# Five buffers of upper weight parts 64 bytes apart modulo 512, lower parts 320 bytes further

## The chip, the cores and the metric

The kernel runs on one core of a Trainium2 chip. The metric is the device time of one execution in microseconds (us). Engines are named as the profile names them: PE is the matrix engine, PEld its loading of stationary operands, DVE the vector engine, ACT the scalar engine, POOL the general engine, SP the engine whose queue issues most of the DMAs. Two runs of the kernel before took 1813.53 and 1813.9 us, median 1813.72 us.

## The reference

One encoder layer in float32 on 256 tokens of width 2048: a half-step feed-forward block, a mixer, a second half-step feed-forward block, each between two RMS norms.

```
D_MODEL = 2048; SEQ = 256; D_FF = 5632; HGRN_WIDTH = 1024; ATTN_WIDTH = 1024; KV_WIDTH = 256
def swiglu(x, w_gate_up, w_down):
    gate, up = jnp.split(x @ w_gate_up, 2, axis=-1)
    return (jax.nn.silu(gate) * up) @ w_down
...
ff = swiglu(rms_norm(x, pre_norm_ffn1), w_ffn1_gate_up, w_ffn1_down)
x = x + 0.5 * rms_norm(ff, post_norm_ffn1)
h = rms_norm(x, pre_norm_mix)
q_h, i_h, f_fwd, f_bwd, g_h, q_a, k_a, v_a = jnp.split(h @ w_mix_in, split_at, axis=-1)
y_h = hgrn2_mixer(q_h, i_h, f_fwd, f_bwd, g_h, ...)      # gated recurrence, chunks of 64 tokens
y_a = window_attention(q_a, k_a, v_a, attn_sink, rel_bias_table)
x = x + rms_norm(concatenate([y_h, y_a]) @ w_mix_out, post_norm_mix)
ff = swiglu(rms_norm(x, pre_norm_ffn2), w_ffn2_gate_up, w_ffn2_down)
x = x + 0.5 * rms_norm(ff, post_norm_ffn2)
```

The weights are read once each; nearly all arithmetic is in the products with the gate/up weights (2048 x 11264), the down weights (5632 x 2048), the mixer's input weights (2048 x 6656) and its output weights (2048 x 2048).

## The kernel before, in words

**Products in three parts.** PE takes float32r operands, which keep fewer bits than float32. So every operand x is split into an upper part (a float32r copy) and a lower part (x minus the upper part), and a product is the sum of three matmuls: upper by upper, upper by lower, lower by upper (`three`, lines 450 to 466, the matmul itself at line 458; `products_N`, lines 375 to 381). In `three` the activations (tiles `xt`, `ht`, `xs`, `sp`, `yh`, `ya`) are stationary and the weight parts (`h`, `l`) stream past them, 512 columns at a time. In the mixer's projections (`proj_T_pieces`, lines 326 and 331) it is the other way about: the weight parts are stationary, 128 columns each, and the activations stream.

**Splitting.** A weight tile arrives by DMA in a `raw` tile of 2048 float32 per partition. Each half of it goes through `split_half` and `split_act`: ACT copies 1024 values into an `h` tile (line 177), DVE subtracts and writes an `l` tile (line 178).

```python
    def split_half(raw, i, hp=hip, lp=lop):
        part = raw[:, i * 1024 : (i + 1) * 1024]
        h = hp.tile([P, 1024], F32R, tag="h", name=nm("h"))
        l = lp.tile([P, 1024], F32R, tag="l", name=nm("l"))
        split_act(h, l, part)
```

The pools `hip` and `lop` have five buffers each, used in turn for the whole kernel. Some of the blocks are multiplied by a Strassen-like scheme of seven products in place of eight (`seven`, `products`), whose first block comes from small tiles elsewhere (`h1`, `l1`, `ha`, `la`, `first`).

**Order of the work.** PE, DVE and ACT run in an order written out by hand (`tc.manual_schedule`). The order in which SP issues the weights' DMAs follows from the buffers that come free.

**Where tiles begin.** Pools lie one after another in a partition of the on-chip memory, and a tile's start is the sum of what was allocated before it. In this text the phase of a tile is its start address in a partition, in bytes, modulo 512. The matmul operands are slices of tiles that begin at multiples of 512 bytes within them, so an operand has its tile's phase. Before the change `X`, the three lasting `raw` buffers, all ten `h` and `l` buffers, `xt`, `ht`, `xs`, `sp`, `h1`, `l1`, `ha` and `la` have phase 64. Two tiles that nothing reads fill space, one of 416 bytes (`line`, in the pool `stat`, which follows `lop`) and one of 416 bytes (`shim`, at the far end). Tiles of the pool `mid`, in which the mixer's own work goes on, have phase 416: among them `kT`, `qh` and the pair `cum0`/`cum1`, which twice holds the parts of a first block (named `first` in the trace). The other `first` tiles have phase 64.

Of the kernel before, what the change touches and what calls it, by code (L numbers as in the profile page):

```python
# [11 lines left out]
F32 = mybir.dt.float32  # L12
# [8 lines left out]
P = 128  # L21
# [12 lines left out]
REL_W = 512  # L34


@with_exitstack
def hymba_layer_kernel(
    ctx: ExitStack,
# [26 lines left out]
    const = ctx.enter_context(tc.tile_pool(name="const", bufs=1))  # L66
    xp = ctx.enter_context(tc.tile_pool(name="xp", bufs=1))
    rawp = ctx.enter_context(tc.tile_pool(name="rawp", bufs=3))
    hip = ctx.enter_context(tc.tile_pool(name="hip", bufs=5))
    lop = ctx.enter_context(tc.tile_pool(name="lop", bufs=5))  # L70
    psum = ctx.enter_context(tc.tile_pool(name="psum", bufs=4, space=bass.MemoryType.PSUM))
    dram = ctx.enter_context(tc.tile_pool(name="dram", bufs=1, space=bass.MemoryType.DRAM))
# [30 lines left out]
    nc.vector.memset(mhalf, -0.5)  # L103
    stat = ctx.enter_context(tc.tile_pool(name="stat", bufs=4))

    stat.tile([P, 104], F32, tag="line", name="line", bufs=1)

    def to_columns(srcs, tag, eng):

# [239 lines left out]
    class LeadN:  # L349


        def __init__(self, w, c0, slot):
            self.w, self.c0, self.slot = w, c0, slot
# [2027 lines left out]
```

## Time and profile before

| what | us |
|---|---|
| median of the runs (two) | 1813.72 |
| span of the profiled execution, first to last instruction | 1810.8 |
| PE busy | 1799.0 (99%) |
| PEld busy | 1494.3 (83%) |
| DVE busy | 1660.0 (92%) |
| ACT busy | 1134.9 (63%) |
| POOL busy | 182.8 (10%) |

How to read it: the span is the time between the first and the last instruction of the profiled execution. The time of a run also holds what lies around the span, 1813.7 - 1810.8 = 2.9 us by the median. The granted PE clock averaged 0.999 of full speed. Matmuls overlap each other, so that a matmul's own duration in a row (some 390 ns) is longer than the step from one matmul's start to the next; the step is what adds up to the span. A row of the timeline or of the chain that holds several matmuls in sequence gives it.

### The profile page before, as it was taken

The numbers are of one execution on the slowest core, as the hardware profiler recorded it, in microseconds if no ns is written. First come the engines' busy times: TensorE is split into PE (matmuls) and PEld (weight loads), VectorE is DVE, ScalarE is ACT, GpSimd is POOL, SyncE is SP. The second block draws the span as 40 slices with busy tenths as digits, with TensorE's granted clock in tenths as the row PEclk, the third lists the DMA queues.
The fourth block names the chain that finished last, engine by engine and source line by source line (L and its number), as shares of the span: only waits on it lengthen the run. The fifth ranks groups of instructions, "written<-read, shape, count | busy, mean of one in ns | idle before, by whom it ended". The sixth has DMA issues, their size and how long they took to land.

```text
span 1810.8 us, 23729 instructions
## 1 busy us (share of the span) xinstructions
PE 1799.0 (99%) x8400; PEld 1494.3 (83%) x8400; DVE 1660.0 (92%) x2179; ACT 1134.9 (63%) x1508; POOL 182.8 (10%) x172
## 2 busy tenths in 40 slices
PE   9999999999999999999999999999999999999998
PEld 7888888888888888888888888888888888888886
DVE  7999999999999998988898898899999999999997
ACT  7565666665665767566676666566666666566663
POOL 1011111111011110110000100111111111011110
PEclk9999999999999999999999999999999999999999
DMA  8889999998699997964655767889999998699994
GB/s 301 248 239 283 273 286 257 248 261 255 214 319 315 301 281 251 296 166 164 175 171 162 243 206 274 256 234 271 284 269 271 255 250 247 190 326 341 270 321 166
DMA packets 218423, 459.16 MB, mean 254 GB/s; under 512 B 13128, under 2 KB 49824, under 8 KB 217024
## 3 DMA queue, kind: packets, MB, share of 16 engines
q1 hardware_dynamic: 181600, 389.07, 61.6%
q0 software_dynamic: 36528, 68.30, 22.1%
q8 instruction: 66, 1.08, 0.2%
q14 instruction: 53, 0.43, 0.1%
q10 hardware_dynamic: 176, 0.27, 0.0%
HBM read 442.89 MB, written 14.70 MB: 253 GB/s over the span
## 4 chain that ended last, share of the span: by engine, by line
PE 96%; DVE 2%; ACT 1%; issue 0%; DMA 0%; DVEq 0%; POOL 0%; ACTq 0%; POOLq 0%
PE pa L458 44%; PE pb L458 38%; PE pa L326 5%; PE pa L331 3%; PE pa L381 1%; PE pa L380 1%; PE pa L379 1%; DVE l L178 1%; PE pb L1728 1%; PE pa L1172 1%; PE pb L1172 1%; PE pb L2029 0%; PE pb L2003 0%; DMA slots<-in_w_mix_out_dram 0%; PE pb L211 0%
## 5 line engine op out<-in xcount | busy, mean ns | idle before, releaser
L177 ACT CAST h<-raw 128x1024 fp32r<-128x1024 f32 (+1 forms) x850 | 835.1, 1012 | 428.2 <-PE pb L458 132.2
L178 DVE TENSOR_TENSOR l<-raw,h 128x1024 fp32r<-128x1024 f32 (+1 forms) x850 | 964.3, 1168 | 76.2 <-ACT h L177 56.4
L458 PE MATMUL pa<-h,xt 128*128 128x512 f32 x1194 | 418.9, 392 | 0.1
L458 PE MATMUL pb<-h,xt 128*128 128x512 f32 x1038 | 371.2, 392 | 0.1
L458 PEld LDWEIGHTS pa<-h,xt 128*128 128x128 f32 x1194 | 224.1, 188 | 48.0 <-DVE xt L233 0.6
L458 PEld LDWEIGHTS pb<-h,xt 128*128 128x128 f32 x1038 | 194.8, 188 | 46.5 <-DVE pb L1236 3.7
L458 PE MATMUL pa<-l,xt 128*128 128x512 f32 x597 | 233.0, 390 | 0.1
L458 PE MATMUL pb<-l,xt 128*128 128x512 f32 x519 | 202.2, 390 | 0.0
L1011 POOL DMA_DIRECT2D raw<-in_w_ffn_gate_up_dram x78 | 94.5, 1212 | 732.0 <-DVE l L178 679.6
L458 PE MATMUL pb<-h,ht 128*128 128x512 f32 x428 | 151.2, 389 | 0.0
L458 PE MATMUL pa<-h,ht 128*128 128x512 f32 x428 | 151.1, 389 | 0.0
L458 PEld LDWEIGHTS pa<-l,xt 128*128 128x128 f32 x597 | 112.2, 188 | 22.7 <-DVE l L178 1.0
L458 PE MATMUL pa<-h,xs 128*128 128x512 f32 x332 | 118.6, 389 | 0.0
L458 PE MATMUL pb<-h,xs 128*128 128x512 f32 x332 | 115.7, 389 | 0.0
L458 PEld LDWEIGHTS pb<-l,xt 128*128 128x128 f32 x519 | 97.5, 188 | 18.7
L326 PE MATMUL pa<-xt,h 128*128 128x512 f32 x448 | 109.9, 393 | 0.0
L326 PEld LDWEIGHTS pa<-xt,h 128*128 128x128 f32 x448 | 81.5, 188 | 15.3
L458 PEld LDWEIGHTS pb<-h,ht 128*128 128x128 f32 x428 | 80.3, 188 | 16.6
L458 PEld LDWEIGHTS pa<-h,ht 128*128 128x128 f32 x428 | 80.3, 188 | 16.6
L1314 POOL DMA_DIRECT2D raw<-in_w_ffn_down_dram x42 | 50.9, 1212 | 367.1 <-DVE la L178 353.7
L458 PE MATMUL pa<-l,ht 128*128 128x512 f32 x214 | 83.3, 389 | 0.0
L458 PE MATMUL pb<-l,ht 128*128 128x512 f32 x214 | 83.3, 389 | 0.0
(341 smaller groups left out, 2583.7 us busy)
## 6 DMA issues: line engine op xcount, KB each, us to landing
raw<-in_w_ffn_gate_up_dram SPq DMA_DIRECT2D x350, 512.0 KB, 5.9
raw<-in_w_ffn_down_dram SPq DMA_DIRECT2D x88, 1024.0 KB, 8.5
raw<-in_w_ffn_gate_up_dram POOLq DMA_DIRECT2D x78, 512.0 KB, 8.2
raw<-in_w_mix_in_dram SPq DMA_DIRECT2D x36, 1024.0 KB, 5.0
raw<-in_w_ffn_down_dram POOLq DMA_DIRECT2D x42, 512.0 KB, 10.2
ht<-away SPq DMA_DIRECT2D x24, 512.0 KB, 10.3
raw<-in_w_mix_out_dram SPq DMA_DIRECT2D x12, 1024.0 KB, 6.5
raw<-in_w_mix_in_dram SPq DMA_DIRECT2D x34, 256.0 KB, 5.6
```

What stands on the lines that cost most here:

```text
L177: nc.scalar.copy(hi, src)
L178: nc.vector.tensor_tensor(lo, src, hi.bitcast(F32), ALU.subtract)
L326: nc.tensor.matmul(slot[f], weights(hs, kk, f), xcol(xt, k), start=(k == 0), stop=(k == KT - 1))
L331: nc.tensor.matmul(slot[f][:, 0:T], weights(ls, kk, f), xcol(xt, kh * 8 + kk, 0), start=False, stop=False,)
L379: nc.tensor.matmul(dst, xh, h[:, o : o + n], start=(k == 0), stop=False)
L380: nc.tensor.matmul(dst, xh, l[:, o : o + n], start=False, stop=False)
L381: nc.tensor.matmul(dst, xl, h[:, o : o + n], start=False, stop=(k == KT - 1))
L458: nc.tensor.matmul(self.bank(at), lhs, rhs, start=(n == 1), stop=n in (ends, self.of[at]), skip_group_check=n > ends,)
L1011: nc.gpsimd.dma_start(raw[:, 0:1024].rearrange("p (k c) -> p k c", k=2), self.source(u, g)[:, :, 1], accum_op=ALU.add,)
L1172: nc.tensor.transpose(bank[:, o : o + P], zs[m][:, k * P : (k + 1) * P], ident)
L1314: nc.gpsimd.dma_start(raws[i][:, 0:1024].rearrange("p (k c) -> p k c", k=2), Pairs.part(w_dn, u, r)[:, :, 512:1024], accum_op=ALU.add,)
L1728: nc.tensor.matmul(dst, left[a], right[b], start=first and i == 0, stop=last and i == 2)
```

## The change

The pool of the upper parts is wrapped, so that each of its five buffers takes 16 float32 (64 bytes) more, of which the tile that is handed out leaves the last 16 unused. A buffer is then 4160 bytes long in place of 4096. The unused tile `line` behind the two pools shrinks by 80 float32 (320 bytes), which is what five buffers grew by.

```diff
+class Stepped:
+    def __init__(self, pool):
+        self.pool = pool
+    def tile(self, shape, *a, **kw):
+        return self.pool.tile([shape[0], shape[1] + 16], *a, **kw)[:, : shape[1]]
...
-    hip = ctx.enter_context(tc.tile_pool(name="hip", bufs=5))
+    hip = Stepped(ctx.enter_context(tc.tile_pool(name="hip", bufs=5)))
     lop = ctx.enter_context(tc.tile_pool(name="lop", bufs=5))
...
-    stat.tile([P, 104], F32, tag="line", name="line", bufs=1)
+    stat.tile([P, 24], F32, tag="line", name="line", bufs=1)
```

What it does to the start addresses (bytes in a partition; phase is modulo 512):

| buffers | before | phase | after | phase |
|---|---|---|---|---|
| `h`, first | 45632 | 64 | 45632 | 64 |
| `h`, second | 49728 | 64 | 49792 | 128 |
| `h`, third | 53824 | 64 | 53952 | 192 |
| `h`, fourth | 57920 | 64 | 58112 | 256 |
| `h`, fifth | 62016 | 64 | 62272 | 320 |
| `l`, all five | 66112 to 82496 | 64 | 66432 to 82816 | 384 |

Every other tile that is read keeps its address. Each engine has the same instructions in the same order, with the same waits; line numbers grow by 10.

## The prediction

> **What bounds the kernel now.** I read the page first, then its chain of waits, then PE's timeline.
>
> ```profile
> PE 1799.0 (99%) x8400; PEld 1494.3 (83%) x8400; DVE 1660.0 (92%) x2179; ACT 1134.9 (63%) x1508; POOL 182.8 (10%) x172
> ...
> PE 96%; DVE 2%; ACT 1%; issue 0%; DMA 0%; DVEq 0%; POOL 0%; ACTq 0%; POOLq 0%
> ```
>
> PE is the bound, in the shares of busy time and in the chain that ended last (96%). So the question is what a matmul's step, from its start to the next one's, will be. The first row below is from the chain, the second from PE's timeline (start, us, what); the two after it are the stretch 500 to 680 us of the windows view and the whole span for line 458.
>
> ```profile
> 152.59 2.72 PE pa L458 x12
> ...
> 821.72 2.08 PE L331 MATMUL pa<-xt,l 128*128 128x256 f32 x16
> ...
> 500.00:680.00 180.00, 180.00 (x795) 148.81 (x794) 171.45 (x205) 116.20 (x141) 24.27 (x20) 1.00 0.98 305
> 0.00:1811.00 1811.00, 1535.69 (x6702) 1251.58 (x6702) 1.00 0.84 254
> ```
>
> Twelve matmuls of 512 columns take 2.72 us, 226.7 ns each; 795 in 180 us give 226.4 ns, while DVE is busy 171.45 us of the 180 and ACT 116.20. Sixteen of 256 columns take 2.08 us, of which the last one's own 0.28 us tail: (2.08 - 0.28) / 15 = 120 ns. So 256 columns more cost 106.7 ns, 512 columns 213.3 ns, and 13.3 ns of each step are fixed. All of this is at phase 64 for both operands. The sum of the whole kernel stands on that step: a nanosecond more on each matmul of line 458 (6702, last row) is 6.7 us.
>
> **The change part by part.** It removes, adds and moves no instruction, no wait and no DMA; SP's and POOL's queues hold the same issues, each as early as the same buffer comes free. It changes phases alone. Counted in the program's list of instructions, 6348 matmuls of 512 columns stream an `h` or `l` buffer of the two pools (6156 of line 458's, 192 of lines 379 to 381): 4232 `h`, 2116 `l`. Of the `h`, 804 fall on the first buffer, which stays. So 3428 + 2116 = 5544 matmuls get a streamed operand at another phase (128, 192, 256, 320 or 384), against stationary operands still at 64. Another 448 + 448 (lines 326 and 331) have them as stationary operand.
>
> *DVE and ACT.* Each half of a weight tile costs one ACT copy and one DVE subtraction, whose source `raw` stays and whose other operands move. The nearest rows in which a destination stands at another phase are the `first` tiles, where one of the five in the first two rows and the one in the last two have phase 416, the others 64 (the columns are least, median and most, in ns):
>
> ```profile
> L177 ACT CAST first<-vr x5: 612/612/622, 721.4 to 783.5; 128x512 fp32r<-128x512 f32 x5
> L178 DVE TENSOR_TENSOR first<-vr,first x5: 680/683/686, 726.4 to 785.9; 128x512 fp32r<-128x512 f32 x5
> ...
> L177 ACT CAST first<-slots x1: 622/622/622, 998.7 to 998.7; 128x512 fp32r<-128x512 f32 x1
> L178 DVE TENSOR_TENSOR first<-slots,first x1: 693/693/693, 999.4 to 999.4; 128x512 fp32r<-128x512 f32 x1
> ```
>
> The spread is 10 and 13 ns at most, so I cost both at nothing. What covers them is PE's own pace: in the stretch 500 to 680 us DVE is idle 180 - 171.45 = 8.55 us, 42 ns for each of its 205 instructions. At 13 ns more on each this is still hidden; past 42 ns DVE would set the pace there.
>
> *PE.* Here the trace has six matmuls of 512 columns that stream an operand at another phase than 64: the two groups of three `first` at phase 416. Each in PE's timeline with its neighbours at phase 64, then what these two names hold in total:
>
> ```profile
> 801.63 0.39 PE L458 MATMUL pb<-h,xt 128*128 128x512 f32 x1
> 801.86 0.87 PE L458 MATMUL pa<-first,xt 128*128 128x512 f32 x3
> 802.56 0.39 PE L458 MATMUL pa<-h,xt 128*128 128x512 f32 x1
> 802.78 0.40 PE L458 MATMUL pa<-l,xt 128*128 128x512 f32 x1
> ...
> 1037.67 0.86 PE L458 MATMUL pa<-first,ya 128*128 128x512 f32 x3
> 1038.38 0.39 PE L458 MATMUL pa<-h,ya 128*128 128x512 f32 x1
> ...
> L458 PE MATMUL pa<-first,xt x15: 389/389/397, 742.8 to 802.3; 128*128 128x512 f32 x15
> L458 PE MATMUL pa<-first,ya x3: 396/396/398, 1037.7 to 1038.1; 128*128 128x512 f32 x3
> ```
>
> From 801.86 to 802.56 and from 1037.67 to 1038.38 pass 1.41 us for six, 235 ns a step: 8.3 ns over 226.7. The twelve `first` at phase 64 have 389 ns as median duration, those at 416 have 396. So a start address can cost something. But 416 lies half way between multiples of 64 (416 = 6 x 64 + 32), while every phase before and after the change is a multiple of 64. Two readings fit these rows: the streamed operand must begin at a multiple of 64 bytes, and then 128 to 384 are as good as 64; or it must stand in some longer period as the stationary operand does, and then they are not. For one matmul the bounds are therefore 0 and +8.3 ns, and below nothing -13.3 ns, if some phases lose the fixed part of the step. I take 0, the value at 64: the only multiple of 64 in the trace has it, and the only slow phase is the one that is no multiple of 64. The sum is 5544 x 0 = 0 on PE, 0 on DVE and ACT; with the profiled span 1810.8 + 0 and 2.9 us around it, the time is the median shown, 1813.7 us; I write 1814.
>
> [...]
>
> **The rivals.**
>
> *Slower: streamed against stationary phase.* The mechanism is that PE's stream of one matmul meets the load of the next one's stationary operand, and that it meets it differently when the phases differ by 64 to 320 bytes. PEld is busy 83% of the span, so every stream has a load beside it. For it speaks that a change from one phase to another leaves a trail: after the 416-phase `kT` matmuls the next eight at phase 64 do not go at 226.7 at once.
>
> ```profile
> 854.12 2.01 PE L326 MATMUL pa<-xt,h 128*128 128x512 f32 x8
> 855.97 1.23 PE L331 MATMUL pa<-xt,l 128*128 128x256 f32 x9
> ```
>
> (855.97 - 854.12) / 8 = 231 ns, 4.6 ns over. After the change each triple goes `h`, `l`, `h`, with another phase each time, so that a trail would never end. Against it speaks that such a trail also follows a late matmul at equal phases, so it need not come from addresses:
>
> ```profile
> 431.77 0.47 PE L458 MATMUL pb<-h,xt 128*128 128x512 f32 x1
> 432.08 0.40 PE L458 MATMUL pb<-l,xt 128*128 128x512 f32 x1
> ...
> 433.24 0.40 PE L458 MATMUL pa<-h,xt 128*128 128x512 f32 x1
> 433.48 0.39 PE L458 MATMUL pa<-l,xt 128*128 128x512 f32 x1
> ```
>
> After the step of 310 ns at 431.77 the durations need until 433.48 to come back to 0.39 us. Price: at 4.6 ns on 6348 matmuls 29 us (1843 us); at 8.3 ns on the 5544 that move 46 us (1860 us). Middle: 37 us, 1851 us. It decides if the period in which phases count is over 64 bytes; with 128 bytes, `l` and the second and fourth `h` (1712) would pay, 3828 x 8.3 = 32 us, which is inside. PE alone would carry it, since the other engines only get more time.
>
> *Faster: some phases lose the fixed part.* If a stream that begins at a multiple of 128 needs one fetch less, the 3828 matmuls at 128, 256 and 384 lose up to 13.3 ns: 51 us, 1763 us. For it: 226.7 = 17 x 13.3 and 120 = 9 x 13.3, as if 512 columns (16 x 128 bytes) that start at 64 touched seventeen pieces. Against it: 416 also touches seventeen and took 235. Then DVE is next: 171.45 of 180 us busy leaves at most 5% in that stretch. [...]
>
> *The change does not do what it says.* The addresses are those of the built program; this I leave without a chance of its own. That DVE slows by over 42 ns gets what is left over.
>
> **How the numbers follow.** No change (within 0.3%): 0.46. Slower by phase against phase: 0.42, between 1820 us (a part of the phases pays) and 1860, a little over in the worst case. Faster: 0.10, from 1763 up. DVE or something unseen: 0.02. The likeliest is no change, 1814 us, with its own range of 1809 to 1819. The range for eight in ten takes that (0.46) and the slower case to 8.3 ns on all that move with a few us for trails at line 326 (448 x 4.6 = 2 us), that is to 1862 (about 0.36 of 0.42): 1809 to 1862. About 2% is what a measurement of this kernel tells from no change: 36 us. Slower by more than that (over 1850) is half of the slower case, 0.21; faster by more (under 1777) is most of the faster one, 0.07; the rest, 0.72, lies within.
>
> **What would show each step.** If I am right, PE's chain pieces of twelve keep 2.72 us, the `h,xt` and `l,xt` matmuls keep 389 ns as median, and the stretch that now runs from 500 to 680 us holds 795 matmuls still. In the slower case these read 393 to 397 ns and 2.78 to 2.82 us, in all stages, while ACT's and DVE's mean durations stay; if only some phases pay, rows of equal name show two durations. In the faster case pieces of twelve fall towards 2.56 us where `l` streams, and DVE's idle time shrinks. DVE's subtraction of 128x1024 at over 1260 ns would prove the term "nothing" on DVE wrong. The forecast fails if phases in multiples of 64 count for PE at all.

## The result and the profile after

The changed kernel takes 1840.72 us (1840.53 to 1840.91, two runs) against 1813.72 us: 1.0146 times as long, 95% interval 1.0116 to 1.0175. That is 27.0 us more. The time lies inside the stated range and within 2%, but the likeliest case, no change, did not happen; the slower rival did, near the lower of its two prices (1843 us). The span is 1839.1 us where it was 1810.8, and the mean granted PE clock is 0.999 as before. Of all executions behind this text, two took more than twice as long as the others of their kernel (3815.85 us of the kernel with the upper parts alone, 3864.56 us of the kernel before): they are left out of every time here, and since the first is the one that was traced, no row of that trace is used.

The page of the changed kernel, busy times and chain; lines are 10 higher than before:

```profile
PE 1827.9 (99%) x8400; PEld 1497.7 (81%) x8400; DVE 1665.5 (91%) x2179; ACT 1135.4 (62%) x1508; POOL 182.8 (10%) x172
...
PE 96%; DVE 2%; DMA 0%; issue 0%; ACT 0%; DVEq 0%; POOL 0%; ACTq 0%; POOLq 0%
```

PE is still the bound with the same 96% of the chain. Its busy time grew by 1827.9 - 1799.0 = 28.9 us, as much as the span (28.3 us); DVE, ACT and POOL stayed within 6 us. Pieces of twelve in the chain of the changed kernel, and its stretch from 500 to 680 us in the windows view (PE, PEld, DVE, ACT, POOL busy and their instructions, then clock, DMA share, GB/s):

```profile
69.27 2.79 PE pa L468 x12
...
79.70 2.79 PE pa L468 x12
...
84.59 2.77 PE pa L468 x12
...
500.00:680.00 180.00, 180.00 (x778) 145.93 (x777) 170.38 (x205) 114.10 (x137) 24.28 (x20) 1.00 0.99 307
```

Twelve matmuls take 2.77 to 2.79 us in place of 2.72. In the same 180 us, PE starts 778 matmuls in place of 795, one each 231.4 ns in place of 226.4, at a clock of 1.00 both times. The groups of instructions, first before, then after (busy us, mean ns of one, idle before):

```profile
L177 ACT CAST h<-raw 128x1024 fp32r<-128x1024 f32 (+1 forms) x850 | 835.1, 1012 | 428.2 <-PE pb L458 132.2
L178 DVE TENSOR_TENSOR l<-raw,h 128x1024 fp32r<-128x1024 f32 (+1 forms) x850 | 964.3, 1168 | 76.2 <-ACT h L177 56.4
L458 PE MATMUL pa<-h,xt 128*128 128x512 f32 x1194 | 418.9, 392 | 0.1
L458 PE MATMUL pa<-h,ht 128*128 128x512 f32 x428 | 151.1, 389 | 0.0
L458 PE MATMUL pa<-l,ht 128*128 128x512 f32 x214 | 83.3, 389 | 0.0
```

```profile
L187 ACT CAST h<-raw 128x1024 fp32r<-128x1024 f32 (+1 forms) x850 | 836.9, 1010 | 448.8 <-PE pb L468 159.2
L188 DVE TENSOR_TENSOR l<-raw,h 128x1024 fp32r<-128x1024 f32 (+1 forms) x850 | 969.2, 1170 | 96.5 <-ACT h L187 78.9
L468 PE MATMUL pa<-h,xt 128*128 128x512 f32 x1194 | 424.4, 396 | 0.1
L468 PE MATMUL pa<-h,ht 128*128 128x512 f32 x428 | 153.2, 394 | 0.0
L468 PE MATMUL pa<-l,ht 128*128 128x512 f32 x214 | 84.2, 393 | 0.0
```

The copies on ACT and the subtractions on DVE kept their means (1012 and 1010 ns, 1168 and 1170 ns) although their destinations moved. The kinds of matmul shown are 4 to 5 ns longer. From the starts of all 512-column matmuls in the two traces (the step of a matmul runs from its start to the next one's; those under 300 ns are counted) the mean step is 227.3 ns before and 231.6 ns after, and in each of eight stages, the same matmuls before and after, it is up by 3.4 to 5.2 ns. All steps of the line that is 458 before, waits included, add up to 1529.5 us before and 1557.4 us after: 27.9 us, nearly the whole loss.

Paired with the program's addresses, the trace says something more: the matmuls on the first `h` buffer, which kept phase 64, have a mean step of 232.4 ns, no less than those on the four that moved (231.7 to 232.6 ns). So a matmul can be slow without having moved. That asked for the experiments.

### The profile page after: what moved, and what is told of

Its sections match the earlier page's. It is cut to its first block, busy times and chain, and to the rows that moved or that the text cites. A ratio compares the mean times of both kernels' runs of the same rounds, so it can differ in the third digit from the quotient of the medians.

```text
span 1839.1 us, 23729 instructions
## 1 busy us (share of the span) xinstructions
PE 1827.9 (99%) x8400; PEld 1497.7 (81%) x8400; DVE 1665.5 (91%) x2179; ACT 1135.4 (62%) x1508; POOL 182.8 (10%) x172
## 4 chain that ended last, share of the span: by engine, by line
PE 96%; DVE 2%; DMA 0%; issue 0%; ACT 0%; DVEq 0%; POOL 0%; ACTq 0%; POOLq 0%
PE pa L468 44%; PE pb L468 39%; PE pa L336 5%; PE pa L341 3%; PE pa L391 1%; PE pa L390 1%; PE pa L389 1%; DVE l L188 1%; PE pb L1738 1%; PE pa L1182 1%; PE pb L1182 1%; PE pb L2039 0%; PE pb L221 0%; DMA slots<-in_w_mix_out_dram 0%; PE pb L2013 0%
## 5 line engine op out<-in xcount | busy, mean ns | idle before, releaser
L187 ACT CAST h<-raw 128x1024 fp32r<-128x1024 f32 (+1 forms) x850 | 836.9, 1010 | 448.8 <-PE pb L468 159.2
L188 DVE TENSOR_TENSOR l<-raw,h 128x1024 fp32r<-128x1024 f32 (+1 forms) x850 | 969.2, 1170 | 96.5 <-ACT h L187 78.9
L468 PE MATMUL pa<-h,xt 128*128 128x512 f32 x1194 | 424.4, 396 | 0.1
```

The source lines that it names most:

```text
L187: nc.scalar.copy(hi, src)
L188: nc.vector.tensor_tensor(lo, src, hi.bitcast(F32), ALU.subtract)
L468: nc.tensor.matmul(self.bank(at), lhs, rhs, start=(n == 1), stop=n in (ends, self.of[at]), skip_group_check=n > ends,)
```

## The experiments

Three theories went into the runs. **Streams in succession** (theory A in the expectations): PE is slow when one matmul's streamed operand has another phase than that of the matmul before it. **Stream against stationary** (theory B): it is slow when the streamed operand has another phase than the stationary one. **Absolute**: some phases of the streamed operand are bad, or good, by themselves. All times are set against runs of the kernel before on the same chip (medians 1814.32, 1813.78 and 1813.87 us in the three batches); ratios have their 95% interval.

Most of the kernels use an unused tile as a spacer, taken back behind the two pools, so that nothing else moves:

```diff
     hip = ctx.enter_context(tc.tile_pool(name="hip", bufs=5))
+    pad = ctx.enter_context(tc.tile_pool(name="pad", bufs=1))
+    pad.tile([P, 80], F32, tag="pad", name="pad")
     lop = ctx.enter_context(tc.tile_pool(name="lop", bufs=5))
...
-    stat.tile([P, 104], F32, tag="line", name="line", bufs=1)
+    stat.tile([P, 24], F32, tag="line", name="line", bufs=1)
```

**Lower parts alone, 320 bytes** (the diff above: `h` stays at 64, `l` goes to 384, as in the change).

> Only the lower parts move, by 320 bytes (phase 384); the upper parts keep phase 64. Theory A (what costs is that a streamed operand stands at another phase than the streamed operand before it): h and l alternate in each triple, so two of three steps change phase as with the change itself, and the time is that of the change, 1835 to 1843 us. Theory B (what costs is that a streamed operand stands at another phase than the stationary operand): only the 2116 matmuls that stream l pay, a third of them: 27 us x 2116 / 5544 = 10 us, 1824 us, and the matmuls that stream h keep a median of 389 ns.

Measured: 1840.81 us, ratio 1.0144 (1.0127 to 1.0161). This half of the change makes the whole loss. Time and `h` rows are as theory A expected; theory B expected 1824 us and `h` rows at 389 ns. Its stretch from 500 to 680 us, and two groups of it:

```profile
500.00:680.00 180.00, 180.00 (x779) 145.76 (x778) 169.99 (x205) 113.80 (x137) 24.28 (x20) 1.00 0.99 306
...
L460 PE MATMUL pa<-h,ht 128*128 128x512 f32 x428 | 152.9, 393 | 0.0
...
L460 PE MATMUL pa<-l,ht 128*128 128x512 f32 x214 | 84.2, 393 | 0.0
```

The `h` matmuls, whose operands are where they were before, went from 389 to 393 ns with the `l` ones. Mean steps over the whole trace: `l` 232.05 ns, unmoved `h` (with `h1`) 231.7 ns, where both had 227.1 to 227.2 before. Every third matmul pairs unlike phases, and the two between pay as well: 2109 x 4.9 = 10 us on `l`, 4425 x 4.5 = 20 us on `h`. Together that is somewhat more than the 26.5 us measured, since PE also waits less: 51 steps of over 300 ns on this line in place of 67.

**Upper parts alone, in steps of 64 bytes** (`lop` placed ahead of the stepped pool, so that `l` stays at 64 while `h` has 64 to 320).

```diff
-    hip = ctx.enter_context(tc.tile_pool(name="hip", bufs=5))
     lop = ctx.enter_context(tc.tile_pool(name="lop", bufs=5))
+    hip = Stepped(ctx.enter_context(tc.tile_pool(name="hip", bufs=5)))
```

> The upper parts begin 64 bytes further each (64, 128, 192, 256, 320), the lower parts stay at phase 64; the two pools change places in memory for that. Theory A: four in five triples still change phase twice, so about four fifths of the change's cost, 22 us, 1835 us. Theory B: 3428 of 5544 matmuls pay, 27 x 0.62 = 17 us, 1830 us, and matmuls that stream l keep 389 ns.

Measured: 1836.67 us, ratio 1.0122 (1.0105 to 1.0139). The other half of the change costs 22.4 us by itself, more than theory B's 17 and close to theory A's 22. The halves do not add up (26.5 + 22.4 against 27.0 us): beside those of one half, the unlike pairs of the other add little.

**Both parts 320 bytes** (the spacer ahead of `hip`: `h` and `l` all at 384).

> Upper and lower parts both move by 320 bytes, so all ten buffers stand at phase 384 and the stationary operands at 64. Theory A: successive streamed operands have the same phase but at the blocks that come from other tiles (some 550 of 6700 matmuls), so 1814 to 1820 us. Theory B: all 6348 matmuls pay, at least the change's 27 us x 6348 / 5544 = 31 us: 1845 us or more, up to 1866 at 8.3 ns each.

Measured: 1836.6 us, ratio 1.0121 (1.0106 to 1.0137), which neither theory expected (A at most 1820 us, B at least 1845). From one matmul to the next the streamed operand now keeps its phase, and the time is nearly as long. So a change of phase between streams is not needed for the loss; what is left for it is that they stand differently from the stationary operand, or that 384 is bad by itself. But the loss is 4.2 us smaller than with the lower parts alone, though three times as many matmuls now pair unlike phases. So not every unlike pair costs the same, and that a change of phase between streams adds something of its own isn't ruled out by any of these runs.

**Lower parts alone, 256 bytes** (spacer of 64 float32, `l` at 320).

> Only the lower parts move, by 256 bytes (phase 320). If phases count modulo 128 or 256 bytes, the time is that of the kernel before, 1814 us, with 389 ns in all rows. If they count modulo 512 or more, it is that of the lower parts moved by 320 bytes, within 3 us.

Measured: 1814.37 us, ratio 1.0001 (0.9992 to 1.0011). Its stretch:

```profile
500.00:680.00 180.00, 180.00 (x795) 148.80 (x794) 172.97 (x207) 116.67 (x140) 24.27 (x20) 1.00 0.98 306
```

795 matmuls, as before the change. 256 bytes cost nothing: the period divides 256.

**Lower parts alone, 128 bytes** (spacer of 32 float32, `l` at 192).

> Only the lower parts move, by 128 bytes (phase 192). If phases count modulo 128 bytes, nothing changes: 1814 us, 389 ns. If they count modulo 256, this is half a period away and costs something else than the move by 320 (which is 64 modulo 256): more or less than its 26.5 us, but not zero, above 1818 us.

Measured: 1828.68 us, ratio 1.0081 (1.0066 to 1.0096): 14.9 us more. So the period is 256 and not 128. The groups:

```profile
L460 PE MATMUL pa<-h,ht 128*128 128x512 f32 x428 | 151.3, 390 | 0.0
...
L460 PE MATMUL pa<-l,ht 128*128 128x512 f32 x214 | 84.4, 394 | 0.0
```

Here only the `l` matmuls are longer, 394 ns beside 390 for `h`. Mean steps over the trace: `l` 233.5 ns, `h` 228.0. At 128 bytes the matmul that pairs unlike phases pays and those between hardly do; at 320 they all did.

**Both parts 128, both parts 64** (the spacer ahead of `hip`; `h` and `l` at 192, then at 128).

> Upper and lower parts both move by 128 bytes (phase 192). Modulo 128: 1814 us. Modulo 256: not zero; like the move of both by 320 bytes (1836.6 us) if any mismatch costs the same, or faster than 1810 us if half a period away the stream and the load of the next stationary operand never meet.

> Upper and lower parts both move by 64 bytes (phase 128). With a period of 128 or 256 bytes this is the same as the move of both by 320: 1836.6 us, within 3 us, with the streams at 393 to 397 ns. With a period of 512 it need not be.

Measured: 1847.85 us, ratio 1.0188 (1.0171 to 1.0205), and 1837.12 us, ratio 1.013 (1.0115 to 1.0145). 64 bytes give what 320 gave (1.0121 with an overlapping interval), as a period of 256 wants, since 320 = 256 + 64. 128 gives the longest time of all runs, longer than either of the two cases expected for it (1836.6 us, or under 1810): its stretch holds 775 matmuls.

```profile
500.00:680.00 180.00, 180.00 (x775) 144.99 (x774) 169.38 (x204) 113.48 (x137) 24.75 (x21) 1.00 0.99 305
```

**Both parts and the far end, 320 bytes** (as both parts 320, and the tiles of the far end too: `xt`, `ha`, `la`, `sp` at 384; `xs` and nearly all of `ht` stay at 64).

```diff
-    shim.tile([P, 104], F32, tag="shim", name="shim")
+    shim.tile([P, 24], F32, tag="shim", name="shim")
```

> All ten buffers at phase 384 as in the move of both by 320, and with them the tiles of the far end (xt, ha, la, sp there, by a smaller unused tile shim): streamed and stationary operands have equal phases again where xt is stationary without xs beside it, and in the mixer's projections; the stationary ht and xs of the feed-forward blocks stay at 64. If only the difference of phases counts (theory B in its bare form), the first group (10 to 60 us) and the mixer's stage go as in the kernel before, steps of 226.7 ns, and the stages with ht (480 to 680, 1570 to 1800 us) go as with both moved by 320, 231 to 233 ns: 1820 to 1832 us. If the phase itself counts (a start at a multiple of 128 bytes is bad whatever the other has), all stages stay slow: 1836 us or more.

Measured: 1824.74 us, ratio 1.0062 (1.0047 to 1.0077). Moving the stationary side after the streamed one takes back half of the loss. Groups of this kernel, `sp` mostly at 384 like the streams, `xs` at 64:

```profile
L460 PE MATMUL pa<-h,xs 128*128 128x512 f32 x332 | 121.2, 397 | 0.0
...
L460 PE MATMUL pa<-h,sp 128*128 128x512 f32 x204 | 71.2, 390 | 0.0
L460 PE MATMUL pa<-l,xs 128*128 128x512 f32 x166 | 65.8, 396 | 0.0
...
L460 PE MATMUL pa<-l,sp 128*128 128x512 f32 x102 | 39.8, 390 | 0.0
```

The same streams at 384 take 390 ns past a stationary operand at 384 and 396 to 397 past those that stayed. By addresses: 3753 matmuls at 384 against 384 have 227.9 ns as mean step, 2521 at 384 against 64 have 230.7. Not all unlike pairs pay the same: with `ht`, `h` had 227.9 and `l` 231.3 ns, where 231 to 233 had been expected of both; why `h` escapes is open. So 384 is not bad by itself.

**The far end alone, 320 bytes** (only `shim` changed). Its mirror image: the streams stay and half of the stationary operands move.

> Only the far end begins 320 bytes further (xt, ha, la, sp at phase 384); h, l, ht, xs and the rest stay at 64. The counterpart of the run that moved both: if the relation counts, the stages that stream h and l past xt are slow (667 matmuls between 60 and 210 us where the kernel before has 677, steps of 230 to 233 ns) and the stage with ht, 500 to 680 us, is back at 795 matmuls and 226.7 ns. 4666 matmuls of 512 columns then pair unlike starts: at 4 to 5 ns each 19 to 23 us, 1833 to 1837 us. If the address of the streamed operand alone counts: no change but for the few tiles that stream from the far end, 1814 to 1818 us.

Measured: 1838.76 us, ratio 1.0137 (1.0122 to 1.0152), somewhat above what was expected: 3764 unlike matmuls on `h` and `l` have a mean step of 233.5 ns, 6 ns over and not 4 to 5. (From 384 to 64 is a distance of -320 bytes, 192 modulo 256, and so another one than that of the streams at 384 against 64.) The stretch with `ht` holds 784 matmuls, not the expected 795, since it also has triples past `sp`, which lies at the far end and was overlooked. There PE's timeline shows the passage:

```profile
559.62 0.39 PE L458 MATMUL pa<-h,sp 128*128 128x512 f32 x1
...
561.72 0.40 PE L458 MATMUL pb<-h,ht 128*128 128x512 f32 x1
561.96 0.39 PE L458 MATMUL pb<-l,ht 128*128 128x512 f32 x1
562.18 0.39 PE L458 MATMUL pb<-h,ht 128*128 128x512 f32 x1
...
563.34 0.39 PE L458 MATMUL pa<-l,ht 128*128 128x512 f32 x1
...
567.87 0.40 PE L458 MATMUL pa<-ha,ht 128*128 128x512 f32 x1
```

Nine matmuls past `sp` (64 against 384) take 2.10 us, 233 ns each. The next seven, past `ht` (64 against 64), take 1.62 us, 231 ns each, and only the twenty after them, in 4.53 us, have 226.5 ns: a trail of some seven matmuls at like phases behind unlike ones. In all 32 places of this trace where at least twelve unlike pairs are followed by twenty like ones, the first seven of these average 231.1 ns, and from the eighth on they have 226.7.

The trace also shows whose stationary operand counts. In this passage the streams stay at 64, and the stationary operand goes from `xs`, at 64, to `xt`, at 384:

```profile
71.89 0.39 PE L458 MATMUL pb<-h,xs 128*128 128x512 f32 x1
...
73.02 0.39 PE L458 MATMUL pb<-h,xs 128*128 128x512 f32 x1
73.25 0.40 PE L458 MATMUL pb<-h,xt 128*128 128x512 f32 x1
...
74.42 0.39 PE L458 MATMUL pa<-h,xt 128*128 128x512 f32 x1
```

Six matmuls past `xs` take 1.36 us, 227 ns each, and the next five, past `xt`, 1.17 us, 234 ns each. The trace has 65 such places, with at least eight like pairs and then eight unlike ones: the last matmul past `xs`, whose successor already has its stationary operand at 384, still has a step of 226.0 ns on average; the first past `xt` has 235.8. By the starts in the trace it is a matmul's own stationary operand that matters, and not the next one's.

**Everything by 64, 32 and 192 bytes** (the spacer ahead of both pools, `line` left as it is, so that all behind it moves too, and `shim` smaller by the same; every matmul of lines 379 to 381 and 458 moves with its partner, and phase 64 becomes 128, 96 and 256).

```diff
+    pad = ctx.enter_context(tc.tile_pool(name="pad", bufs=1))
+    pad.tile([P, 16], F32, tag="pad", name="pad")
     hip = ctx.enter_context(tc.tile_pool(name="hip", bufs=5))
...
-    shim.tile([P, 104], F32, tag="shim", name="shim")
+    shim.tile([P, 88], F32, tag="shim", name="shim")
```

> All tiles that PE reads begin 64 bytes further (128 in place of 64 modulo 512, and those of the pool mid 480 in place of 416); nothing stands differently to anything else. If only the start of the streamed operand relative to the stationary one counts, modulo 256 bytes: no change, 1814 us, within 2 us, 795 matmuls in the stretch 500 to 680 us. If the start itself counts, as in the rival in which streams at multiples of 128 lose the fixed part of the step: up to 13.3 ns less on some 7000 matmuls, DVE next, some 1750 to 1765 us. If a start at 128 is as bad by itself as it was when only h and l stood there: 1837 us.

> As the run before, with 32 bytes in place of 64, so that no operand begins at a multiple of 64 (96 modulo 512). If only the relative start counts: 1814 us, within 2 us. If a start must be a multiple of 64, as the prediction's value of nothing supposed: 235 ns a step on some 7300 matmuls, 8.3 x 7300 = 61 us, 1875 us, 766 matmuls in the stretch 500 to 680 us.

> As the two before, with 192 bytes: all starts at multiples of 256. Relative start: 1814 us, within 2 us. If a row that begins on a boundary of 256 bytes saves a piece: faster, down to 1760 us.

Measured: 1814.32 us, ratio 1.0004 (0.9994 to 1.0013); 1814.28 us, 0.9999 (0.999 to 1.0009); 1814.33 us, 1.0004 (0.9995 to 1.0013). Nothing, three times. The absolute theory falls: 128 is as good for all as 64, 96 is no worse though it is no multiple of 64, 256 is no better. From the run with 32 bytes, the stretch, and the `first` tiles by their durations (least, median, most, ns):

```profile
500.00:680.00 180.00, 180.00 (x795) 148.84 (x794) 172.95 (x207) 115.94 (x140) 24.27 (x20) 1.00 0.98 305
...
L460 PE MATMUL pa<-first,xt x15: 389/389/397, 744.5 to 804.0; 128*128 128x512 f32 x15
L460 PE MATMUL pa<-first,ya x3: 396/396/397, 1039.2 to 1039.7; 128*128 128x512 f32 x3
```

The two groups of three `first` from the pool `mid` now begin at 448, a multiple of 64, and are as slow as at 416: 396 to 397 ns, mean step 234.7 ns. They stand 352 bytes from their stationary operands, as before.

## Why the prediction was right and wrong

**What bounds the kernel**: right. PE's step makes the loss, and the sum per nanosecond (6.7 us on line 458) turns the measured 4.3 ns into 29 us, beside 28.3 us of span measured.

**DVE and ACT, 0**: right; 1168 to 1170 ns and 1012 to 1010 ns.

**PE, "I take 0"**: the step that failed. The six slow `first` matmuls were read rightly as an effect of a start address, and both readings that fit them were written down. The choice between them rested on 416 being no multiple of 64. The run at 96 throughout (1814.28 us) shows that multiples of 64 have no part in it, and the `first` tiles at 448 are as slow. What those rows and 64 against 64 had apart was not only 416 in itself but its distance from the stationary operand, 352 bytes, and the trace of before holds no row at another distance that is a multiple of 64. "The only multiple of 64 in the trace has it" was true, but that multiple was also the only like pair: the two readings were confounded, and the row chosen as "nearest" spoke for neither. So the term 5544 x 0 was wrong in both factors: a matmul cost 4.3 ns and not 0, and it was not only the 5544 that moved, since those on the first `h` buffer, which stayed, went to 232.4 ns with the others. It measured 27.9 us on line 458.

**The slower rival**: its condition ("if the period in which phases count is over 64 bytes") was met; the period is 256 bytes, as far as distances were tried (`l` moved by 256 bytes 1814.37 us, by 128 bytes 1828.68). Its lower price, 4.6 ns on 6348 matmuls, 29 us, came from the trail behind the `kT` matmuls and was close, with 27.0 us measured, though nothing then said that a trail at other distances would have that size; its signs came too, with 393 to 396 ns in most rows and 2.77 to 2.79 us for twelve; the higher, 8.3 ns on the 5544 that move, was not reached, and its middle of 1851 us was 10 too high. That a trail would never end is what the lower parts alone showed: unmoved `h` matmuls at 231.7 ns. But the reason given, another phase at each matmul of a triple, was wrong in part: with both parts at 384 the streamed phase stays the same, and the loss is nearly as large. The variant with a period of 128 is refuted. The rival's mechanism was a stream that meets the load of the next matmul's stationary operand. That the two operands' relation counts is shown; but where own and next differ, in the kernel with the far end alone, the step follows the matmul's own stationary operand (226.0 against 235.8 ns). So that part of the mechanism isn't borne out, and what happens inside PE stays open.

**The faster rival**: refuted by its own mechanism, not only by the time. With everything at 128 or at 256 no fixed part was lost (1814.32 and 1814.33 us). So 226.7 = 17 x 13.3 did not count pieces that a better start would save.

**The chances**: 0.46 for no change and 0.42 for slower named two readings as about equally likely, which the rows allowed; 1840.72 us lies in the range because it was drawn over both. That it lies there is luck as far as the forecast of 1814 us goes: the reason given for that value did not hold.

**The two operands**: they are not indifferent to each other. With both parts and the far end moved by 320 bytes, the same streams at 384 take 227.9 ns a step past stationary operands at 384 and 230.7 past those at 64, and the time follows (1824.74 us, against 1836.6 with the far end left where it was).

## What to carry to other kernels

Where float32r matmuls run back to back and PE is the bound, let the streamed and the stationary operands begin at the same address modulo 256 bytes; here unlike starts cost 0.6 to 1.9%, and the place itself, tried by moving everything by 32, 64 and 192 bytes, nothing (ratios 0.9999 to 1.0004). A small unused tile of 64 bytes ahead of the two pools was enough to lose 1.3%, and buffers of 4160 bytes in place of 4096, for the upper parts alone, to lose 1.2%; a smaller unused tile at the far end took back half of the loss of both parts at 320 bytes (ratio 1.0062 in place of 1.0121). Only this kernel was tried, with 512 columns streamed against 128 loaded. When a few slow rows stand out by an address, ask what else is different in them, above all relative to the partner operand, before taking the reading that costs nothing.

## What had not been expected of the hardware

- The step depends on the distance of the two operands modulo 256 bytes, as far as distances were tried: as means over the trace, 0 and 256 give 227.3 ns; 64 and 320 for both parts 231.1; 128 for both 232.6; the unlike pairs at -320, which is 192, have 233.5; six at 352 about 235 (the `first` tiles of the kernel before, and of that with everything 32 bytes further).
- An unlike pair slows its neighbours. With `l` alone 320 bytes off, the `h` pairs beside it, which are like, run at 231.7 ns; with `l` alone 128 bytes off they run at 228.0. Why 128 leaves a shorter trail stays open.
- The loss does not add up: 26.5 us for `l` alone, 22.4 for `h` alone, 27.0 for both; and 22.3 for both at the same 320 bytes.
- DVE and ACT show no such effect: in the changed kernel the tiles that they write stand at six phases, and the mean durations moved by 2 ns.

Distances that are no multiple of 32 were not tried, and no run changed the phase from one stream to the next while every pair stayed alike, which would show what such a change costs by itself. No phase tried was faster than equal ones, so the kernel before remains the best of these.
